# Stores issued from GpSimd, and twelve prepended rows left out of the later stages, in a hybrid decoder layer on one Trainium2 core

## The chip, the cores and the metric

The kernel runs on one core of one Trainium2 chip. A core has four compute engines that run side by side, each with its own in-order queue of instructions: TensorE (PE, matrix products into PSUM), VectorE (DVE), ScalarE (ACT) and GpSimd (POOL). SyncE (SP) computes nothing; it issues DMAs between HBM and SBUF. Engines wait for one another by semaphores. The metric is the device time of one execution in microseconds; several executions are timed and the median is compared.

## The reference, cut to what matters

One layer of a decoder trunk with 1024 channels is applied to a prompt of 2048 rows, preceded by 16 learned "meta" rows, and to 8 sample sequences of 8 rows each with stored histories. All in float32. In short:

```
h    = rmsnorm(x)                       # per row, 1024 channels
z    = h @ w_in                         # 1024 -> 5 x 1024: value, gate, pool input, two merge gates
a    = value * sigmoid(gate)            # then causal depthwise convolution, width 31, layernorm, silu, @ w_conv_out
p    = trailing mean over 2/4/8/16 rows of the pool input, minus the row itself; small products, scale
x    = x + (sigmoid(g_a) * a + sigmoid(g_b) * p) @ w_out
up   = rmsnorm(x) @ w_up                # 1024 -> 2 x 2816, causal depthwise convolution, width 3
x    = x + (gelu(up_gate) * up_value) @ w_down
y    = rmsnorm(x)                       # y_prompt = y[:, 16:], the 16 meta rows are dropped
```

Beside y, the last rows of each history are returned (30 of the width-31 convolution, 15 of the pooling, 2 of the width-3 convolution), for the prompt and for the samples. What a row needs from earlier rows is thus: 30 rows of `a`, 15 rows of the pool input, 2 rows of `up`. The first row of y that is kept is row 16.

## The kernel before

**Layout.** Channels lie on the 128 partitions, in 8 chunks; rows are columns. All rows, 16 + 2048 + 64 = 2128, are cut into three blocks (`NBLK`, `WIDTHS`, lines 33 to 41) of 708, 708 and 712 columns; the 64 sample rows are the last columns of block 2. A block is computed in two halves of `hw(b)` = 354 or 356 columns (lines 229 to 241), since a PSUM bank holds 512 float32 columns.

**Products.** Precision is kept by splitting both operands in a high and a low part: `gemm` (line 331) issues three matmuls for each chunk of 128 input channels and each half, so a unit of 1024 input channels is 8 x 2 x 3 = 48 matmuls. Every matmul goes through the helper at line 212. The up-projections stream two columns more per half (the history of the width-3 convolution). In block 2, 19 of the 22 pairs of up-projections are computed by a recursive scheme with 7 products of half size instead of 8 (`pair`, line 964).

**Weights.** A weight tile is loaded (`raw`), split by ScalarE and VectorE into a tile `wb` with both parts (`w_split`, line 293), and, if a later block needs it, stored to a DRAM tile `keep` (`w_stores`, line 270). Later uses load the split form from `keep` (`w_loads`, line 275). There are four `wb` buffers; a `wb` buffer is loaded or written again when TensorE has read it and its store has landed. The sums and differences of weights that block 2's scheme needs are prepared during block 1 and kept in the same way (`mixed_weights`, line 867: 14 stores for each of 19 pairs).

**Order.** The order of all instructions is written out by the program itself, under `manual_schedule`: a planner (`Pace`, line 71) keeps, for each engine and for the DMA, the time at which it would be free, and every helper reports a cost to it (`pace.put`). The list of units is walked in order; after each unit's matmuls, `drip` (line 1442) lets evacuations, weight splits and tasks (norms, convolutions) issue instructions until VectorE's planned time comes near TensorE's. Some tasks also hold back while the planned DMA time is ahead of TensorE's (`calm`, lines 882 and 1091). Each engine then executes its own instructions in the order in which they were issued.

**Queues.** All loads (line 204) and all stores (line 208) are issued by SyncE, in one queue. GpSimd makes small copies only (`pcopy`, line 200): the last rows of a block into the histories `ahist`, `phist`, `hhist`, and from there to the head of the next block's tiles.

**Stages of a block.** `G` (gate and value inputs), `PG` (pool input, pool products, merge gate), `C` (second merge gate, convolution's output product), `WO` (output projection), `FF` (up-projections with down-projections between them). In `value_post` (line 527) the tile of `a` has its 30 history columns ahead of the block's own; in `pool_post` (line 670) the pool tile has 15. For the first 16 rows the trailing mean is corrected by a table of counts (lines 707 to 710). `final` (line 1085) normalizes and stores y. All 2128 rows go through all stages.

Of the kernel before, what the change touches and what calls it, by code (L numbers as in the profile page):

```python
# [9 lines left out]
F32R = mybir.dt.float32r  # L10
# [4 lines left out]
P = 128  # L15
# [18 lines left out]
SBLK = 2  # L34
TOT = NP_ALL + NSAMP
_W = TOT // NBLK // 4 * 4
# [96 lines left out]
def trunk(ctx: ExitStack, tc: tile.TileContext, A, O):  # L133
# [73 lines left out]
    def store(dst, src):  # L207
        nc.sync.dma_start(out=dst, in_=src)  # L208
        pace.put("dma", size(src) * P * 4 / 340.0, [], [src], late=2000.0)

# [15 lines left out]
    def hcol(o):  # L226
        return half[:, o - O_LG : o - O_LG + 1]

    def hw(b):
        return WIDTHS[b] // 2  # L230

    def cols(b, ts_):
# [7 lines left out]
    def ps_of(ps, b, ts_, off=0):  # L240
        return ps[:, : len(ts_), off : off + hw(b)]

    R = {}
# [100 lines left out]

    def rng(b, ts_, halo=0):
        h = hw(b)
        return [(t * h, (t + 1) * h + halo) for t in ts_]

# [76 lines left out]
    def x_load(b, c, c0=0, c1=None):  # L425
        c1 = WIDTHS[b] if c1 is None else c1
        x = S(c1 - c0)
        load(x, A["x"][c, :, COL0[b] + c0 : COL0[b] + c1])
        return x
# [18 lines left out]
    def norm1_first(ts_):  # L448

        c0, c1 = cols(0, ts_)  # L450
        xs = [x_load(0, c, c0, c1) for c in range(KC)]
        yield at(xs[0])

        def src(c):
            yield
            return xs[c]

        r = yield from rstd_of(src, c1 - c0)
        if ts_[0] == 0:
            R["h", 0] = [(S(WIDTHS[0], F32R), S(WIDTHS[0], F32R)) for _ in range(KC)]  # L460

        def first(c):
            stt(xs[c], xs[c], col(O_N1 + c), r, ALU.mult, ALU.mult)
            act(R["h", 0][c][0][:, c0:c1], xs[c], AF.Copy)
            return xs[c], *(x[:, c0:c1] for x in R["h", 0][c])

        yield from staggered(first)
# [53 lines left out]
    def gate_post(b, c, ts_, ps):  # L521
        if ts_[0] == 0:
            R["t", b, c] = S(WIDTHS[b])
        act(sb(R["t", b, c], b, ts_), ps_of(ps, b, ts_), AF.Tanh, scale=0.5)
        yield

    def value_post(b, c, ts_, ps):
        n, h, t = NPB[b], hw(b), R["t", b, c]
        if ts_[0] == 0:
            a = S(HC + n)  # L530
            pcopy(a[:, :HC], ahist[:, c, :])
            R["a", b, c] = [a, None, 0]
        a = R["a", b, c][0]
        if n == WIDTHS[b]:
            stt(sb(a[:, HC:], b, ts_), sb(t, b, ts_), 1.0, ps_of(ps, b, ts_), ALU.add, ALU.mult)
        else:
            s = R["sa", c]
            stt(a[:, HC : HC + h], t[:, :h], 1.0, ps[:, 0, :h], ALU.add, ALU.mult)
            stt(a[:, HC + h : HC + n], t[:, h:n], 1.0, ps[:, 1, : n - h], ALU.add, ALU.mult)
            new = t[:, n:].rearrange("p (a c) -> p a c", a=NS)  # L540
            stt(new, new, 1.0, ps[:, 1, n - h : h].rearrange("p (a c) -> p a c", a=NS), ALU.add, ALU.mult)
            ts(s[:, :, HC:], new, 0.5, None, ALU.mult)
            store(O["conv_s"][c], s)
            R["a", b, c][1] = 1
        if ts_[-1] == 1:
            pcopy(ahist[:, c, :], a[:, n : n + HC])
            R["a", b, c][2] = 1
            del R["t", b, c]
        yield
# [120 lines left out]
    def pool_post(b, c, ps):  # L670
# [3 lines left out]
        u = S(HP + n)  # L674
        pcopy(u[:, :HP], phist[:, c, :])
        if samp:
# [5 lines left out]
        else:  # L682
            act(sb(u[:, HP:], b, BOTH), ps_of(ps, b, BOTH), AF.Copy)
        pcopy(phist[:, c, :], u[:, n : n + HP])
# [22 lines left out]
        if b == 0:  # L707
            e = mpool.tile([P, 16], F32, tag="e", name=nm("e"), bufs=2)
            tt(e, cur[:, HP : HP + 16], cst[:, O_IC + 16 * g : O_IC + 16 * g + 16], ALU.mult)
            tt(pf[:, :16], e, u[:, HP : HP + 16], ALU.subtract)  # L710
        hi, lo = S(W, F32R), S(W, F32R)
# [420 lines left out]

    def std_unit(w, pairs, b, ts_, post, needs=(), wait=False, halo=0, pre=None, drop=None, hold=None):
        box = []

        def mmf(w):
            if pre:
                pre()
            ps = hold.pop() if hold else PSUM()
            (box if hold is None or ts_ == SECOND else hold).append(ps)  # L1140
            yield from gemm(ps if hold is None else ps[:, ts_[0] :, :], w, pairs(), rng(b, ts_, halo))
            if drop:
                del R[drop]
# [8 lines left out]
    def gate(b, c, w, nd, ts_=BOTH):  # L1152
        std_unit(w, lambda: R["h", b], b, ts_, lambda ps: gate_post(b, c, ts_, ps), nd)

    def value(b, c, w, nd, ts_=BOTH, drop=False):
        std_unit(
            w, lambda: R["h", b], b, ts_, lambda ps: value_post(b, c, ts_, ps), nd,
            pre=past(b, "sa", c, HC, "st_conv", 3), drop=("h", b) if drop else None,
        )
# [44 lines left out]
    def in_unit(b, part, c, post, nd, pre=None, drop=None):  # L1204
        std_unit(
            W(("in", part * KC + c), A["w_in"][part * KC + c]), lambda: R["h", b], b, BOTH, lambda ps: post(b, c, ps), nd, pre=pre, drop=drop
        )
# [391 lines left out]
```

## Time and profile before

| | us |
|---|---|
| median of 3 runs | 3002.06 (3000.92 to 3005.93) |
| the profiled execution's own time | 3004.2 |
| its span, first to last instruction | 3002.1 |

The profile is one execution. Its page shows how long each engine was busy, what ended idle times ("releaser"), the chain of work that ended last, the instructions in groups (out <- in, partitions x elements, count, total and mean time) and the DMA issues with their time to landing. In the names, `ps` is PSUM, `s` a slot of the working pool, `wb` a split weight, `raw` a weight as loaded, `keep` the split weights in DRAM, `xd` block 2's rows that are spilled to DRAM, `in_` and `out_` the kernel's inputs and outputs. PEld is TensorE's loading of the stationary operand, which overlaps its products. SPq is SyncE's queue.

Over the span the core moved 660.41 MB by DMA, 433.35 MB read from HBM and 224.17 MB written, a mean of 220 GB/s; the granted clock of TensorE was 0.993 of full speed on the mean. A matmul's time in the groups is its time from start to end; matmuls overlap, so it is about twice the interval from one to the next.

### The profile page before, as it was taken

How to read it: one execution, taken by the hardware profiler on the slowest of the kernel's cores; microseconds unless marked ns; L12 is line 12 of the kernel's file. 1: busy time of each engine (PE TensorE's matmuls, PEld its weight loads, DVE VectorE, ACT ScalarE, POOL GpSimd, SP SyncE). 2: the span in 40 equal slices, each digit the busy share in tenths (PEclk: the TensorE clock that was granted, in tenths of full speed). 3: DMA queues.
4: the chain of work that ended last, by engine and by line, in shares of the span. 5: the costliest groups of instructions: out<-in, count | busy, mean ns of one | idle time of the engine just before them, and what ended most of it. 6: DMA issues, size and time to landing. Idle time of an engine off the chain costs nothing.

```text
span 3002.1 us, 44205 instructions
## 1 busy us (share of the span) xinstructions
PE 2938.3 (98%) x17928; PEld 2924.6 (97%) x17928; DVE 2042.8 (68%) x3006; ACT 821.2 (27%) x1238; POOL 108.8 (4%) x201
## 2 busy tenths in 40 slices
PE   7999999999999998999999999999999999999998
PEld 7999999999999998999999999999999999999997
DVE  7998998679996456653489999655652137544645
ACT  4201334233223232432221212223241113221312
POOL 0111100020000000000010000000000000000000
PEclk9999999999999999999999999999999999999999
DMA  7424554955655557888743444799743376777686
GB/s 283 160 71 161 196 207 162 335 212 173 229 189 197 204 191 286 274 321 277 277 154 120 163 136 146 266 320 328 266 170 138 139 267 215 255 268 263 236 302 242
DMA packets 187755, 660.41 MB, mean 220 GB/s; under 512 B 30880, under 2 KB 39200, under 8 KB 145696
## 3 DMA queue, kind: packets, MB, share of 16 engines
q1 hardware_dynamic: 187552, 657.59, 62.2%
q8 instruction: 141, 2.31, 0.3%
q14 instruction: 62, 0.51, 0.0%
HBM read 433.35 MB, written 224.17 MB: 219 GB/s over the span
## 4 chain that ended last, share of the span: by engine, by line
PE 81%; DVE 12%; ACT 2%; DMA 2%; issue 2%; SPq 0%; DVEq 0%; ACTq 0%
PE ps L212 81%; DVE s L184 8%; DVE s L180 2%; DVE wb L180 2%; ACT s L195 2%; DMA wb<-keep 1%; DMA s<-in_x 0%; ACT wb L195 0%; DMA out_ffn_s<-sf 0%; DMA raw<-in_w_in 0%; SPq L204 0%; DVE s L189 0%; DMA raw<-in_w_dn 0%; SPq L208 0%; DVE rs L184 0%
## 5 line engine op out<-in xcount | busy, mean ns | idle before, releaser
L212 PE MATMUL ps<-s,wb 128*128 128x356 f32 (+2 forms) x17628 | 2904.4, 326 | 32.3 <-DMA wb<-keep 11.7
L212 PEld LDWEIGHTS ps<-s,wb 128*128 128x128 f32 x17628 | 2886.3, 189 | 43.2 <-DVE s L180 19.4
L184 DVE SCALAR_TENSOR_TENSOR s<-s,half,s 128x708 f32<-128x708 f32 (+1 forms) x720 | 622.5, 928 | 0.0
L195 ACT ACTIVATE s<-s 128x708 fp32r<-128x708 f32 (+8 forms) x447 | 316.2, 715 | 829.9 <-DVE s L184 465.8
L180 DVE TENSOR_TENSOR s<-s,s 128x708 f32<-128x708 f32 (+10 forms) x526 | 402.4, 779 | 102.5 <-ACT s L195 92.7
L180 DVE TENSOR_TENSOR s<-s,ps 128x708 f32<-128x708 f32 (+4 forms) x225 | 159.7, 719 | 289.9 <-PE ps L212 233.5
L195 ACT ACTIVATE s<-ps 128x358 f32<-128x358 f32 (+4 forms) x197 | 117.5, 603 | 696.4 <-PE ps L212 679.8
L184 DVE SCALAR_TENSOR_TENSOR s<-ps,cst,s 128x708 f32<-128x708 f32 (+1 forms) x188 | 179.0, 953 | 91.6 <-ACT s L195 88.0
L184 DVE SCALAR_TENSOR_TENSOR s<-s,cst,s 128x712 f32<-128x712 f32 (+3 forms) x188 | 156.5, 845 | 88.2 <-ACT s L195 81.0
L180 DVE TENSOR_TENSOR wb<-raw,wb 128x1024 fp32r<-128x1024 f32 (+3 forms) x136 | 152.9, 1126 | 41.0 <-ACT wb L195 40.6
L195 ACT ACTIVATE wb<-raw 128x1024 fp32r<-128x1024 f32 (+3 forms) x136 | 132.2, 977 | 157.4 <-PE ps L212 92.3
L195 ACT ACTIVATE s<-ps,cst 128x708 f32<-128x708 f32 (+1 forms) x94 | 79.4, 847 | 272.9 <-PE ps L212 266.5
L184 DVE SCALAR_TENSOR_TENSOR s<-s,ps 128x708 f32<-128x708 f32 (+5 forms) x65 | 43.8, 695 | 144.1 <-PE ps L212 124.8
L184 DVE SCALAR_TENSOR_TENSOR s<-s,s 128x708 f32<-128x708 f32 (+2 forms) x96 | 85.5, 891 | 73.4 <-ACT s L195 71.6
L180 DVE TENSOR_TENSOR s<-raw,s 128x512 fp32r<-128x512 f32 x114 | 74.5, 687 | 60.8 <-ACT s L195 52.5
L195 ACT ACTIVATE s<-raw 128x512 fp32r<-128x512 f32 x114 | 68.2, 626 | 86.9 <-DMA raw<-in_w_up 68.7
L180 DVE TENSOR_TENSOR s<-s 128x722 f32<-128x722 f32 (+6 forms) x64 | 55.3, 863 | 28.2 <-ACT s L195 20.5
L200 POOL COPY s<-phist 128x15 f32<-128x15 f32 x24 | 16.5, 687 | 1080.4 <-PE ps L212 1023.8
L184 DVE SCALAR_TENSOR_TENSOR sc<-sa,cst,sc 128x64 f32<-128x64 f32 x232 | 46.9, 280 | 0.3
L195 ACT ACTIVATE s<-s,half 128x708 f32<-128x708 f32 (+1 forms) x48 | 46.5, 975 | 0.8
L195 ACT ACTIVATE s<-s,cst 128x712 f32<-128x712 f32 x38 | 33.7, 886 | 40.4 <-DVE s L180 38.4
L200 POOL CAST s<-hhist 128x2 fp32r<-128x2 f32 x48 | 17.5, 396 | 607.8 <-PE ps L212 389.8
(51 smaller groups left out, 369.5 us busy)
## 6 DMA issues: line engine op xcount, KB each, us to landing
wb<-keep SPq DMA_DIRECT2D x227, 1024.0 KB, 5.0
keep<-wb SPq DMA_DIRECT2D x100, 1024.0 KB, 6.3
keep<-s SPq DMA_DIRECT2D x266, 256.0 KB, 5.7
raw<-in_w_up SPq DMA_DIRECT2D x82, 512.0 KB, 5.7
wb<-keep SPq DMA_DIRECT2D x40, 640.0 KB, 5.2
wb<-keep SPq DMA_DIRECT2D x32, 768.0 KB, 5.2
raw<-in_w_in SPq DMA_DIRECT2D x40, 512.0 KB, 5.2
s<-in_x SPq DMA_DIRECT2D x40, 354.0 KB, 7.6
```

What stands on the lines that cost most here:

```text
L180: nc.vector.tensor_tensor(out=out, in0=a, in1=b, op=op)
L184: nc.vector.scalar_tensor_tensor(out=out, in0=a, scalar=s, in1=b, op0=op0, op1=op1)
L195: nc.scalar.activation(out, a, func, **kw)
L200: nc.gpsimd.tensor_copy(out, a)
L212: nc.tensor.matmul(out, lhsT=lhsT, rhs=rhs, start=start, stop=stop, skip_group_check=again)
```

## The change

Two edits are made together.

First, `store` issues its DMA from GpSimd in place of SyncE. To the planner a store is now an instruction of GpSimd of 1000 ns whose source is free 2000 ns and the transfer's time later; the DMA's planned time grows by the transfer alone and no longer waits for the store's source.

Second, the first 12 of the 16 meta rows (`SKIP`) go only through what later rows need of them: the gate and value inputs and the pool input of block 0. Of a first row kept in the other stages, row 12, the convolution reaches back 30 rows, so `a` of rows 0 to 11 is still computed; it is written into the history columns ahead of the block's own (`HC - lead(b)`), and the same holds for the pool input. The blocks become 704, 704 and 708 columns wide. Block 0's gate, value and pool units stream both halves of 716 columns, 358 each (`hx`, `rows="all"`); its merge gates start at column 12 of the normalized rows (`rows="h"`).

```diff
-TOT = NP_ALL + NSAMP
+SKIP = 12
+TOT = NP_ALL + NSAMP - SKIP
...
     def store(dst, src):
-        nc.sync.dma_start(out=dst, in_=src)
-        pace.put("dma", size(src) * P * 4 / 340.0, [], [src], late=2000.0)
+        nc.gpsimd.dma_start(out=dst, in_=src)
+        move = size(src) * P * 4 / 340.0
+        pace.put("pool", 1000.0, [], [src], late=2000.0 + move)
+        pace.free["dma"] += move
...
+    def lead(b):
+        return SKIP if b == 0 else 0
+    def hx(b):
+        return (WIDTHS[b] + lead(b)) // 2
+    def sx(ap, b, ts_):
+        return ap[:, ts_[0] * hx(b) : (ts_[-1] + 1) * hx(b)].rearrange("p (a c) -> p a c", a=len(ts_))
+    def px_of(ps, b, ts_):
+        return ps[:, : len(ts_), : hx(b)]
...
-    def rng(b, ts_, halo=0):
-        h = hw(b)
-        return [(t * h, (t + 1) * h + halo) for t in ts_]
+    def rng(b, ts_, halo=0, rows="own"):
+        h = hx(b) if rows == "all" else hw(b)
+        o = lead(b) if rows == "h" else 0
+        return [(o + t * h, o + (t + 1) * h + halo) for t in ts_]
...
     def value_post(b, c, ts_, ps):
-            pcopy(a[:, :HC], ahist[:, c, :])
+            pcopy(a[:, : HC - lead(b)], ahist[:, c, : HC - lead(b)])
...
-            stt(sb(a[:, HC:], b, ts_), sb(t, b, ts_), 1.0, ps_of(ps, b, ts_), ALU.add, ALU.mult)
+            stt(sx(a[:, HC - lead(b) :], b, ts_), sx(t, b, ts_), 1.0, px_of(ps, b, ts_), ALU.add, ALU.mult)
...
     def pool_post(b, c, ps):
-        pcopy(u[:, :HP], phist[:, c, :])
+        pcopy(u[:, : HP - lead(b)], phist[:, c, : HP - lead(b)])
...
-            act(sb(u[:, HP:], b, BOTH), ps_of(ps, b, BOTH), AF.Copy)
+            act(sx(u[:, HP - lead(b) :], b, BOTH), px_of(ps, b, BOTH), AF.Copy)
```

In the same way the loads of x and the normalized tiles of block 0 (`x_load`, `norm1_first`) take the 12 rows in, the table of counts is read from entry 12 on, and `gate`, `value` and the pool inputs pass `rows="all"`, block 0's merge gates `rows="h"`. On the host, x keeps all rows and the output y has 12 rows fewer.

More of the change, by code (lines that the diff above doesn't have):

```diff
@@ L427, in x_load @@
         x = S(c1 - c0)
-        load(x, A["x"][c, :, COL0[b] + c0 : COL0[b] + c1])
+        load(x, A["x"][c, :, SKIP + COL0[b] + c0 : SKIP + COL0[b] + c1])
         return x
@@ L448, in norm1_first @@
     def norm1_first(ts_):
-        c0, c1 = cols(0, ts_)
-        xs = [x_load(0, c, c0, c1) for c in range(KC)]
+        c0, c1 = ts_[0] * hx(0), (ts_[-1] + 1) * hx(0)
+        xs = [x_load(0, c, c0 - SKIP, c1 - SKIP) for c in range(KC)]
         yield at(xs[0])
@@ L459, in norm1_first @@
         if ts_[0] == 0:
-            R["h", 0] = [(S(WIDTHS[0], F32R), S(WIDTHS[0], F32R)) for _ in range(KC)]
+            R["h", 0] = [(S(2 * hx(0), F32R), S(2 * hx(0), F32R)) for _ in range(KC)]
         def first(c):
@@ L522, in gate_post @@
         if ts_[0] == 0:
-            R["t", b, c] = S(WIDTHS[b])
-        act(sb(R["t", b, c], b, ts_), ps_of(ps, b, ts_), AF.Tanh, scale=0.5)
+            R["t", b, c] = S(2 * hx(b))
+        act(sx(R["t", b, c], b, ts_), px_of(ps, b, ts_), AF.Tanh, scale=0.5)
         yield
@@ L708, in pool_post @@
             e = mpool.tile([P, 16], F32, tag="e", name=nm("e"), bufs=2)
-            tt(e, cur[:, HP : HP + 16], cst[:, O_IC + 16 * g : O_IC + 16 * g + 16], ALU.mult)
-            tt(pf[:, :16], e, u[:, HP : HP + 16], ALU.subtract)
+            k = 16 - SKIP
+            tt(e[:, :k], cur[:, HP : HP + k], cst[:, O_IC + 16 * g + SKIP : O_IC + 16 * g + 16], ALU.mult)
+            tt(pf[:, :k], e[:, :k], u[:, HP : HP + k], ALU.subtract)
         hi, lo = S(W, F32R), S(W, F32R)
@@ L1131, in add_task, with std_unit @@
         order.append(t)
-    def std_unit(w, pairs, b, ts_, post, needs=(), wait=False, halo=0, pre=None, drop=None, hold=None):
+    def std_unit(w, pairs, b, ts_, post, needs=(), wait=False, halo=0, pre=None, drop=None, hold=None, rows="own"):
         box = []
@@ L1140, in mmf @@
             (box if hold is None or ts_ == SECOND else hold).append(ps)
-            yield from gemm(ps if hold is None else ps[:, ts_[0] :, :], w, pairs(), rng(b, ts_, halo))
+            yield from gemm(ps if hold is None else ps[:, ts_[0] :, :], w, pairs(), rng(b, ts_, halo, rows))
             if drop:
@@ L1152, in gate @@
     def gate(b, c, w, nd, ts_=BOTH):
-        std_unit(w, lambda: R["h", b], b, ts_, lambda ps: gate_post(b, c, ts_, ps), nd)
+        std_unit(w, lambda: R["h", b], b, ts_, lambda ps: gate_post(b, c, ts_, ps), nd, rows="all")
     def value(b, c, w, nd, ts_=BOTH, drop=False):
@@ L1157, in value @@
             w, lambda: R["h", b], b, ts_, lambda ps: value_post(b, c, ts_, ps), nd,
-            pre=past(b, "sa", c, HC, "st_conv", 3), drop=("h", b) if drop else None,
+            pre=past(b, "sa", c, HC, "st_conv", 3), drop=("h", b) if drop else None, rows="all",
         )
@@ L1205, in in_unit @@
         std_unit(
-            W(("in", part * KC + c), A["w_in"][part * KC + c]), lambda: R["h", b], b, BOTH, lambda ps: post(b, c, ps), nd, pre=pre, drop=drop
+            W(("in", part * KC + c), A["w_in"][part * KC + c]), lambda: R["h", b], b, BOTH, lambda ps: post(b, c, ps), nd, pre=pre, drop=drop,
+            rows="all" if part == 2 else "h",
         )
@@ L1542 @@
     samp = I["x_sample"].reshape(NSAMP, D)
-    cut = sum(NPB[: SBLK + 1])
+    cut = SKIP + sum(NPB[: SBLK + 1])
     x = np.concatenate([prompt[:cut], samp, prompt[cut:]], axis=0)
@@ L1559 @@
     arrays = {
-        "x": x.T.reshape(KC, P, TOT),
+        "x": x.T.reshape(KC, P, SKIP + TOT),
         "cst": cst,
@@ L1582 @@
     y = o["y"].reshape(D, TOT).T
-    yp = np.concatenate([y[N_META:cut], y[cut + NSAMP :]], axis=0)[None]
+    cut -= SKIP
+    yp = np.concatenate([y[N_META - SKIP : cut], y[cut + NSAMP :]], axis=0)[None]
     ys = y[cut : cut + NSAMP].reshape(NS, TS, D)
```

## The prediction

> **What bounds the kernel now.** I read the busy shares first, then the matmul groups by shape, then windows inside single stages, then who waits for whom (TensorE, the DMA queue of SyncE, GpSimd), then the chain of waits around the longest stalls and at the end.
>
> ```profile
> span 3002.1 us, 44205 instructions
> PE 2938.3 (98%) x17928; PEld 2924.6 (97%) x17928; DVE 2042.8 (68%) x3006; ACT 821.2 (27%) x1238; POOL 108.8 (4%) x201
> L212 PE MATMUL ps<-s,wb 128*128 128x356 f32 x8064 | 1327.0, 326 | 7.2 <-ACT s L195 3.1 <-DVE s L184 1.5 <-DVE s L180 1.3
> L212 PE MATMUL ps<-s,wb 128*128 128x354 f32 x7680 | 1265.6, 327 | 14.9 <-DMA wb<-keep 9.6 <-ACT s L195 4.3 <-DVE s L180 1.0
> L212 PE MATMUL ps<-s,wb 128*128 128x358 f32 x1884 | 315.6, 328 | 10.2 <-DVE s L180 8.5 <-DMA wb<-keep 1.7
> ```
>
> TensorE is the bound: 17628 matmuls of 354 to 358 columns, with 64 us of idle time in the whole span. So the change can pay in two ways only: a shorter interval between matmuls, or fewer stalls. The windows below lie inside stages without a stall; their columns are length, busy time with count, granted clock, DMA share and GB/s.
>
> ```profile
> 1200.00:1400.00 200.00, 200.00 (x1229) 1.00 0.88 308
> 2200.00:2410.00 210.00, 210.00 (x1295) 1.00 0.38 139
> 785.00:861.00 76.00, 76.00 (x465) 1.00 0.54 187
> 2774.00:2845.00 71.00, 68.50 (x412) 1.00 0.71 249
> ```
>
> One matmul lasts about 0.326 us and overlaps the next, so the interval is (window + 0.326) over the count: 163.0 ns at 354 columns (block 1's projections), 162.4 at 356 in block 2's projections, 164.1 at 356 in the up-projections of block 0. In the last window, the 358-column products of block 2, 2.5 us are idle and every wait is followed by a refill, so 167 ns is an upper figure.
>
> The stalls that a DMA ends are few:
>
> ```profile
> PE ps L212 <- DVE s L180: 28.0, 24, 10.2
> PE ps L212 <- DMA wb<-keep: 11.7, 4, 7.5
> ```
>
> The longest of them, in the chain of waits, with the two windows that follow it and a window around the second one (windows of all engines: PE, PEld, DVE, ACT, POOL, then clock and DMA):
>
> ```profile
> 1178.97 9.32 DMA wb<-keep
> 1188.29 0.14 issue
> 1188.43 6.67 PE ps L212 x23
> 1184.00:1194.00 10.00, 5.57 (x19) 5.60 (x20) 7.72 (x10) 3.38 (x6) 2.05 (x4) 0.51 1.01 420
> 2111.00:2121.00 10.00, 7.95 (x50) 7.68 (x49) 10.00 (x13) 4.95 (x8) 0.00 (x0) 1.00 1.00 342
> ```
>
> The reader should see two things. The load that TensorE waits for took 9.32 us, and the granted clock fell to 0.51 after the long stall: 23 matmuls took 6.67 us where 23 x 0.163 = 3.7 us is normal, so 2.9 us more were lost. After a stall of about 2 us (second window) the clock stayed at 1.00.
>
> **The change, part by part.**
>
> *Fewer columns.* Blocks go from 708, 708, 712 columns to 704, 704, 708. Blocks 0 and 1 have 3840 matmuls each that go from 354 to 352 columns and 2112 up-projections that go from 356 to 354; block 2 has 3840 from 356 to 354 and 1884 from 358 to 356. Against this, block 0's gate, value and pool inputs keep the 12 rows: 24 units of 48 matmuls, 1152, go from 354 to 358. In columns streamed: 16476 x 2 = 32952 fewer, less 1152 x 4 = 4608 more, 28344 in all. The number of matmuls does not change.
>
> The price of a column is not plain from the trace. From 354 (163.0) to the up-projections' 356 (164.1) it is 0.55 ns; from 354 to block 2's 356 (162.4) it is -0.3 ns; an interval wholly in proportion to its columns gives 163.0/354 = 0.46. I take 0.4, near the last two positive ones: 28344 x 0.4 = **-11.3 us**. Bounds: -0.3 gives +8.5, 0.55 gives -15.6. VectorE and ScalarE lose 4 of 708 columns as well; they are 68% and 27% busy and lie beside the matmuls, so I count nothing.
>
> *Stores leave SyncE's queue.* Waits of that queue, stores being line 208:
>
> ```profile
> SPq L208 <- ACT s L195: 141.3, 73, 5.8
> SPq L208 <- DVE wb L180: 92.9, 10, 15.9
> SPq L208 <- DVE s L180: 87.1, 95, 5.0
> SPq L204 <- PE ps L212: 1141.5, 275, 27.1
> SPq L204 <- DVE wb L180: 685.1, 116, 24.9
> ```
>
> Three groups of stores hold the head of the queue for 321 us in all, and loads stand behind them. But loads (line 204) wait far more for TensorE and for the weight splits, that is, for their own buffers. So most of the head-of-line time is hidden, and what can come back is what TensorE loses to DMA. Around the stalls the queue looks like this (the last two lines are the load of the fourth stall in the chain of waits, and the loads' median time to landing):
>
> ```profile
> 1176.66 1.33 SPq L204 DMA_DIRECT2D raw<-in_w_up  x2
> 1178.04 0.53 SPq L208 DMA_DIRECT2D keep<-wb  x1
> 1178.97 7.24 SPq L204 DMA_DIRECT2D wb<-keep  x4
> 2107.32 1.05 SPq L208 DMA_DIRECT2D keep<-s  x2
> 2108.43 2.77 SPq L204 DMA_DIRECT2D s<-in_x  x4
> 2111.55 7.47 SPq L204 DMA_DIRECT2D wb<-keep  x4
> 2163.23 6.70 SPq L208 DMA_DIRECT2D out_y<-s  x8
> 2170.02 5.38 SPq L204 DMA_DIRECT2D wb<-keep  x3
> 2479.08 6.47 DMA wb<-keep
> wb<-keep SPq DMA_DIRECT2D x227, 1024.0 KB, 5.0
> ```
>
> At 1178.97 the load is issued as its buffer comes free and shares the engines with a 1 MB store and two loads that had stood behind stores; the median landing of such a load is 5.0 us, so 9.32 - 5.0 = 4.3 us can go, and with a shorter stall some of the 2.9 us of slow clock; I take half, 1.5. At 2111 stores held the queue between two groups of x loads, and at 2170 eight stores of y stood ahead of the load. These two and the fourth stall (ended at 2485, beside eight stores of x) hold 11.7 - 7.5 = 4.2 us; I take half, 2.1. Sum: **-7.9 us**. Bounds: 11.7 + 2.9 = -14.6, and on the other side +4.3, if a load that now starts beside a store is held up by as much as the worst one was. What is late next after these stalls is VectorE (28.0 us above), which the change does not touch.
>
> *Stores join GpSimd's queue.* No row shows a DMA issued there. The rows are the two large groups of stores as SyncE issues them (shortest, median and longest issue in ns, first and last start), their landing, a window of block 0, the nearest GpSimd rows, and the end: eight y stores issued in 3.82 us beside the eight VectorE instructions of 4.05 us that feed them.
>
> ```profile
> L208 SPq DMA_DIRECT2D keep<-s x266: 319/408/1999, 1157.0 to 2160.7; - x133
> L208 SPq DMA_DIRECT2D keep<-wb x136: 319/432/1767, 16.3 to 1178.0; - x136
> keep<-wb SPq DMA_DIRECT2D x100, 1024.0 KB, 6.3
> 250.00:500.00 250.00, 250.00 (x1540) 249.56 (x1539) 222.48 (x273) 89.21 (x109) 21.81 (x21) 1.00 0.55 194
> L200 POOL COPY phist<-s 128x15 f32<-128x15 f32 x24 | 19.0, 792 | 238.7 <-ACT s L195 148.2 <-ACT su L195 90.4
> L200 POOL CAST s<-s 128x2 fp32r<-128x2 f32 x16 | 5.3, 355 | 52.2 <-ACT s L195 38.8 <-issue 5.4 <-DVE s L180 4.9
> L200 POOL COPY ahist<-s 128x30 f32<-128x30 f32 x24 | 16.7, 694 | 362.2 <-DVE s L184 362.2
> 2994.94 4.05 DVE L184 SCALAR_TENSOR_TENSOR s<-s,cst,ps 128x356 f32<-128x356 f32 x8 [1.75 <-PE ps L212]
> 2995.55 3.82 SPq L208 DMA_DIRECT2D out_y<-s  x8
> ```
>
> Bounds for one issue: 0.32 us (SyncE's shortest) and 1.4 us (twice a 0.69 us copy); I take 0.8, the row of the 0.79 us copy. The groups of stores of line 208 add up to 529 (the 266 and 136 here and 127 smaller ones), so 529 x 0.8 = 423 us beside the 109 that GpSimd is busy now: it stays under a fifth and is no bound on the mean. At the end nothing hides it: the last eight y stores come every 0.5 us and would leave every 0.8, 8 x 0.3 = 2.4, and with a slower start of the last one I take **+3 us** (bounds 0 and 8 x 0.9 = +7).
>
> Elsewhere a store waits in order behind small copies, and copies behind stores. The copies behind which a store can be stuck longest are those of `ahist`, waiting for VectorE: 362.2 us over 24, 15 us each. The buffers that wait for the stores are the four of `wb`, read by TensorE in units of 48 x 0.163 = 7.8 us; a buffer is written again some three units later, so a store has about 20 us, of which 6.3 go to landing. In block 2's hand-over to the up-projections GpSimd has 16 casts and 8 spill stores, 16 x 0.36 + 8 x 0.8 = 12 us, beside 72 matmuls of the first half, 11.7 us, that hide it. I count **+2 us** for this (bounds 0, and the slower rival below).
>
> Sum against the profiled execution's own time, 3004.2 us (span 3002.1 and 2.1 around it): -11.3 - 7.9 + 3 + 2 = -14.2, so 2990.0. That execution lies 2.1 us above the median of the runs, 3002.06, so the forecast for the median is **2988 us**.
>
> **The rivals.**
>
> *The interval does not follow the columns* (weight loading or a fixed turn sets it). For it: block 2's 356 columns are no slower than 354. Against it: the up-projections in the same block and the 358 group, both slower. Then -7.9 + 3 + 2 = -3: **2999 us**.
>
> *The place of the columns counts, not only their number.* Blocks 0 and 1 now start their second half at column 354, block 2 at 356, a multiple of four; the change swaps this (352 there, 354 here). The two 356-column windows differ by 1.7 ns and differ in just this. Then 10752 matmuls gain 1.7 ns more, 1884 products of block 2 too, and 3840 lose it: -18.3 - 3.2 + 6.5 = -15 beside the forecast: **2973 us**.
>
> *The stalls stay,* because those loads waited for a buffer and then for bandwidth, which stores take from whichever queue. For it: 1141.5 us of loads waiting for TensorE, and DMA shares of 1.00 in the windows of both stalls. Then -11.3 + 3 + 2 = -6.3: **2996 us**. The Trainium skill says so as a rule (DMA: Bandwidth & Descriptors, section "Issuing engines are not separate DMA queues"): DMAs of all issuing engines run on the same 16 engines, and a second one saves only issue time; by it this rival is the likelier. The trace agrees as far as the 1.00 goes, but shows the order of the queue as well.
>
> *Slower: stores come late through GpSimd and hold `wb` buffers.* Place: block 0, where most of the 136 stores of new weights fall and VectorE, 222 of 250 us busy in the window above, keeps `ahist` copies waiting. It decides once a store stands more than the spare 20 - 6.3 = 13.7 us behind a copy. The copies' mean wait is 15 us and the longest 48.9; if five of 24 hold a store 5 us too long, TensorE loses 25 us: -11.3 - 7.9 + 3 + 2 + 25 = +11, **3013 us**. Against it: the program issues a copy at about the time its input is planned, and loads have lived with the same order on SyncE. The Trainium skill adds a cause (SBUF — State Buffer, the box on the "DVE blocks DMA" trap): descriptors of DMAs from GpSimd can't be written while VectorE runs a two-port instruction; no run here shows it so far.
>
> **How the numbers follow.** Forecast 2988 (own range 2980 to 2996): 0.42. Fixed interval, 2999: 0.17. Place of the columns, 2973: 0.11. Stalls stay, 2996: 0.13, half of it on either side of the bound. Late stores, 3013: 0.17. About 0.2% (6 us) is what a measurement of this kernel can tell from no change: faster by more (under 2996) 0.42 + 0.11 + 0.07 = 0.60, within 0.2% 0.17 + 0.06 = 0.23, slower 0.17. The range is 2971 to 3010: it leaves out the upper part of the slower case and the lower edge of the fastest.
>
> **What would show it.** The matmul groups by shape: the 352 group's interval near 162.2 ns and block 0's 358 near 164.6 show the column price; 161 or less at 352 shows the place. TensorE's wait for `wb<-keep` under 5 us and no clock of 0.5 near 1184 show the stalls gone. GpSimd's busy time near 530 us shows 0.8 us per issue; the last y store's issue after the last VectorE instruction shows the tail. The prediction is wrong if new waits of TensorE for a DMA or a split appear in block 0, or if the interval does not move.

## The result, and the profile after

| | before | after |
|---|---|---|
| median, us | 3002.01 (3000.92 to 3005.93) | 2983.88 (2982.72 to 2986.44) |
| ratio of the medians | | 0.9938, 95% interval 0.9921 to 0.9956 |
| the profiled execution's own time | 3004.2 | 2985.0 |
| its span | 3002.1 | 2983.2 |

The time fell by 18.1 us where 14 were forecast. The total is near, but two terms of the sum are far off and cancel in part. From here on the change shifts the lines: a matmul is line 215, a load 205, a store 209, a GpSimd copy 201, a ScalarE operation 196, VectorE's two main forms 181 and 185.

The page after (busy time, share and count of each engine):

```profile
span 2983.2 us, 44492 instructions
PE 2918.1 (98%) x17928; PEld 2906.2 (97%) x17928; DVE 2034.3 (68%) x3006; ACT 817.5 (27%) x1238; POOL 380.2 (13%) x730
```

The matmuls of the changed kernel grouped by shape (busy time, mean ns of one, then idle time before them and its releasers):

```profile
L215 PE MATMUL ps<-s,wb 128*128 128x354 f32 x8064 | 1319.3, 325 | 10.4 <-DMA wb<-keep 6.6 <-ACT s L196 1.4 <-DVE s L181 1.3
L215 PE MATMUL ps<-s,wb 128*128 128x352 f32 x6528 | 1060.7, 324 | 9.9 <-ACT s L196 9.7 <-DVE s L181 0.3
L215 PE MATMUL ps<-s,wb 128*128 128x356 f32 x1884 | 314.9, 328 | 12.3 <-DVE s L181 9.1 <-DMA wb<-keep 3.2
L215 PE MATMUL ps<-s,wb 128*128 128x358 f32 x1152 | 197.3, 332 | 4.0 <-ACT s L196 3.4 <-DVE s L181 0.5
```

The counts by width are the ones that the prediction worked out; TensorE is still 98% busy. The mean of 324 to 332 ns hardly moves, since matmuls overlap; what moved is how many fit into a stretch. Three windows of the changed kernel inside stages without a stall (length, then each engine's busy time with its count, clock, DMA share, GB/s):

```profile
213.00:279.00 66.00, 66.00 (x415) 66.00 (x414) 57.85 (x68) 8.59 (x10) 9.01 (x13) 1.00 0.45 162
1200.00:1400.00 200.00, 200.00 (x1244) 200.00 (x1243) 104.03 (x140) 73.30 (x106) 55.07 (x104) 1.00 0.85 302
2200.00:2400.00 200.00, 200.00 (x1237) 199.97 (x1235) 56.33 (x75) 46.18 (x62) 2.29 (x8) 1.00 0.42 153
```

The second window holds 1244 matmuls of 352 columns where it held 1229 of 354: (200 + 0.326)/1244 = 161.0 ns against 163.0. The first is the clearest place. In the kernel before, the same stretch (block 1's gate and value products) was:

```profile
213.00:279.00 66.00, 66.00 (x407) 66.00 (x406) 56.98 (x66) 8.61 (x10) 7.34 (x10) 1.00 0.40 144
```

407 products of 354 columns, 163.0 ns each, became 415 of 352, 159.8 ns: 3.2 ns for two columns.

To add this up over the span I took from both traces, for each width, the mean of all start-to-start intervals under 222 ns (longer ones are stalls or slow clock) times the number of products:

```
            352            354            356            358           sum, us
before       -        7680 x 162.91  8064 x 163.16  1884 x 164.66   2877.1
after   6528 x 160.73 8064 x 162.31  1884 x 162.35  1152 x 164.14   2853.1
```

**-24.0 us** come from the intervals. The span fell by 18.9, so all the rest together *rose* by 5.1: the time from the start of the last large product to the end of the span went from 13.8 to 16.2, and the excess in stretches of half clock from about 8 to about 12. TensorE's stalls come to about 50 us in both kernels; they, its small products and the start make up the difference, and how it splits between them depends by some 2 us on the way of counting.

GpSimd's two large groups of stores in the changed kernel (busy time, mean ns of one, then idle time before them):

```profile
L209 POOL DMA_DIRECT2D keep<-s x266 | 142.3, 540 | 640.4 <-ACT s L196 507.8 <-DVE s L181 108.1 <-issue 19.3
L209 POOL DMA_DIRECT2D keep<-wb x136 | 77.1, 567 | 690.0 <-DVE wb L181 673.6 <-DVE rs L192 8.4 <-DVE s L185 6.8
```

Who TensorE waits for there (total, times, longest):

```profile
PE ps L215 <- DVE s L181: 23.5, 22, 9.6
PE ps L215 <- ACT s L196: 14.5, 6, 7.2
PE ps L215 <- DMA wb<-keep: 9.8, 4, 4.9
```

An issue costs 0.54 to 0.57 us, not 0.8. The wait for loads seems to have shrunk a little, from 11.7 to 9.8. But the longest stall has only changed its name. The timeline around it (start, length, instruction, idle time before it):

```profile
1161.13 0.54 POOL L209 DMA_DIRECT2D keep<-s  x1 [0.38 <-issue]
1161.80 0.67 POOL L209 DMA_DIRECT2D keep<-wb  x1
1163.95 19.67 SPq L205 DMA_DIRECT2D wb<-keep  x5
1173.06 11.18 PE L215 MATMUL ps<-s,wb 128*128 128x352 f32 x54 [7.24 <-ACT s L196]
```

The 7.24 us are put down to ScalarE, whose last operation ended at 1172.95. The load of the same weights, issued at 1163.95 just behind a store of a split weight from GpSimd (which landed at 1173.70), landed at 1172.93 by its DMA record: 9.0 us, as before (9.32). Both ended within 0.02 us of one another, so this row alone cannot tell which of them was waited for; the experiment with a quiet hand-over, below, does. The stall is the one forecast to shrink, and it did not.

### The profile page after: what moved, and what is told of

Read it like the earlier page. It is cut to its first block, busy times and chain, and to the rows that moved or that the text cites. A ratio compares the mean times of both kernels' runs of the same rounds, so it can differ in the third digit from the quotient of the medians.

```text
span 2983.2 us, 44492 instructions
## 1 busy us (share of the span) xinstructions
PE 2918.1 (98%) x17928; PEld 2906.2 (97%) x17928; DVE 2034.3 (68%) x3006; ACT 817.5 (27%) x1238; POOL 380.2 (13%) x730
## 4 chain that ended last, share of the span: by engine, by line
PE 85%; DVE 6%; issue 3%; DMA 3%; ACT 2%; POOL 1%; SPq 0%; DVEq 0%; POOLq 0%; ACTq 0%
PE ps L215 85%; DVE s L185 4%; DVE s L181 1%; DMA wb<-keep 1%; ACT s L196 1%; DVE wb L181 1%; POOL keep L209 1%; DMA raw<-in_w_in 1%; DMA raw<-in_w_up 0%; DMA s<-in_x 0%; DMA keep<-s 0%; ACT wb L196 0%; DMA raw<-in_w_out 0%; SPq L205 0%; DVE s L190 0%
## 5 line engine op out<-in xcount | busy, mean ns | idle before, releaser
L215 PE MATMUL ps<-s,wb 128*128 128x354 f32 (+3 forms) x17628 | 2885.0, 325 | 36.5 <-ACT s L196 14.5
L185 DVE SCALAR_TENSOR_TENSOR s<-s,half,s 128x704 f32<-128x704 f32 (+1 forms) x720 | 619.6, 925 | 0.0
L196 ACT ACTIVATE s<-s 128x704 fp32r<-128x704 f32 (+10 forms) x447 | 314.6, 711 | 808.2 <-DVE s L185 455.9
L181 DVE TENSOR_TENSOR s<-s,s 128x704 f32<-128x704 f32 (+11 forms) x526 | 400.7, 775 | 98.3 <-ACT s L196 89.9
L181 DVE TENSOR_TENSOR s<-s,ps 128x704 f32<-128x704 f32 (+4 forms) x225 | 158.8, 715 | 288.8 <-PE ps L215 246.8
L196 ACT ACTIVATE s<-ps 128x356 f32<-128x356 f32 (+5 forms) x197 | 117.0, 600 | 683.7 <-PE ps L215 650.7
L185 DVE SCALAR_TENSOR_TENSOR s<-ps,cst,s 128x704 f32<-128x704 f32 (+1 forms) x188 | 178.2, 949 | 110.9 <-ACT s L196 107.2
L209 POOL DMA_DIRECT2D keep<-s x266 | 142.3, 540 | 640.4 <-ACT s L196 507.8
L185 DVE SCALAR_TENSOR_TENSOR s<-s,cst,s 128x708 f32<-128x708 f32 (+4 forms) x188 | 156.0, 842 | 88.0 <-ACT s L196 82.0
L185 DVE SCALAR_TENSOR_TENSOR s<-s,s 128x704 f32<-128x704 f32 (+2 forms) x96 | 85.2, 888 | 70.9 <-ACT s L196 68.2
```

The lines of the kernel that those rows point to most:

```text
L181: nc.vector.tensor_tensor(out=out, in0=a, in1=b, op=op)
L185: nc.vector.scalar_tensor_tensor(out=out, in0=a, scalar=s, in1=b, op0=op0, op1=op1)
L196: nc.scalar.activation(out, a, func, **kw)
L209: nc.gpsimd.dma_start(out=dst, in_=src)
L215: nc.tensor.matmul(out, lhsT=lhsT, rhs=rhs, start=start, stop=stop, skip_group_check=again)
```

## The experiments

Every ratio is against runs of the kernel before on the same chip; brackets are 95% intervals. First, the two halves of the change by themselves, and the queue apart from the planner's account of it.

**Stores alone.** The kernel before, with the whole of the new `store`; all 2128 rows go everywhere.

```diff
-        nc.sync.dma_start(out=dst, in_=src)
-        pace.put("dma", size(src) * P * 4 / 340.0, [], [src], late=2000.0)
+        nc.gpsimd.dma_start(out=dst, in_=src)
+        move = size(src) * P * 4 / 340.0
+        pace.put("pool", 1000.0, [], [src], late=2000.0 + move)
+        pace.free["dma"] += move
```

> The kernel before with its stores issued from GpSimd and planned as in the change; all 2128 rows stay. Theory A (the gain of 18 us is all in the matmul intervals, about -22 us, and moving the stores costs about 3 us, most of it at the end): 3002 + 3 = 3005 us, steady intervals as before (163.0 ns at 354 columns), stalls for wb<-keep still about 10 us. Theory B (the steps of the forecast: columns about -11, stalls -8, tail and queue +5): about 2999 us, stalls under 5 us.

Measured: 3006.50 us, ratio 1.0015 [1.0006, 1.0024]: about 5 us slower. The stalls stayed: TensorE waits 15.0 us for loads of weights where it waited 11.7, and the longest of these waits is 6.6 us where it was 7.5. About 2 us of the loss lie at the end, where the time from the start of the last large product went from 13.8 to 15.9.

**Rows alone.** The changed kernel with the old `store`.

```diff
-        nc.gpsimd.dma_start(out=dst, in_=src)
-        move = size(src) * P * 4 / 340.0
-        pace.put("pool", 1000.0, [], [src], late=2000.0 + move)
-        pace.free["dma"] += move
+        nc.sync.dma_start(out=dst, in_=src)
+        pace.put("dma", size(src) * P * 4 / 340.0, [], [src], late=2000.0)
```

> The changed kernel with its stores put back on SyncE and planned as before; the 12 rows stay left out. Theory A: 2984 - 3 = 2981 us, intervals as in the changed kernel (about 160.9 ns at 352, 162.3 at 356). Theory B: 3002 - 11 = 2991 us.

Measured: 2985.22 us, 0.9945 [0.9933, 0.9958]. Nearly the whole gain of the change is here. The two halves do not add up: +4.9 and -16.4 make -11.5, together they gave -18.1. So the stores' edit costs time in one kernel and next to nothing in the other. Nor do the rows keep all that the intervals give them: by the sum used above these fell by 24.9 us here (to 2852.2), but TensorE stands 4.6 us near 2157 and 2.2 us near 551, where the kernel before has no stall over 1.1 us. The stores' edit has two parts, and the next run separates them.

**Only the queue back.** The changed kernel, with the new account and thus the new order of VectorE's, ScalarE's and TensorE's instructions, but the DMA issued by SyncE.

```diff
-        nc.gpsimd.dma_start(out=dst, in_=src)
+        nc.sync.dma_start(out=dst, in_=src)
```

> The changed kernel with the one call in store put back on SyncE, but planned as a GpSimd store: TensorE, VectorE and ScalarE get the very instructions of the changed kernel in the same order, only the queue of the stores differs. Theory A: the end comes 2.4 us earlier and the stalls stay near 18 us: about 2981 us. Theory B (the queue of SyncE held loads back): stalls grow by about 8 us: about 2990 us.

Measured: 2977.73 us, 0.9917 [0.9903, 0.9930]. GpSimd's queue, which the change introduces, *costs* about 6 us (the two 95% intervals, 0.9921 to 0.9956 with it and 0.9903 to 0.9930 without, just overlap, so the size is rough; where the time goes is traced below); the new account, at 2985.22 - 2977.73 = 7.5 us, pays. Where it pays most is seen in the chain of waits at about 900 us, in the kernel with rows alone (where a matmul is line 213) and then in this one:

```profile
895.40 0.90 DVE s L181
896.30 0.14 issue
896.44 8.63 PE ps L213 x37
```

```profile
875.00 30.14 PE ps L215 x183
```

With the old account the chain runs over VectorE from 875 to 896, TensorE stands 4.9 us, and 37 products then take 8.63 us where 37 x 0.163 = 6.0 is normal. With the new one TensorE is never without work there. The account changes when the planner hands VectorE's instructions out; no queue is involved.

**The account alone, all rows.** The kernel before with the new account and stores on SyncE.

```diff
-        pace.put("dma", size(src) * P * 4 / 340.0, [], [src], late=2000.0)
+        move = size(src) * P * 4 / 340.0
+        pace.put("pool", 1000.0, [], [src], late=2000.0 + move)
+        pace.free["dma"] += move
```

> The kernel before (all 2128 rows, stores on SyncE) with the planner's new account of a store alone; against e1_stores_only only the queue of the stores differs, the other engines' instructions are the same. Theory (the queue costs 4 to 6 us here as well): 3001 us. Rival (the queue is free, and e1's loss came from the new plan): 3006 us.

Measured: 3001.54 us, 1.0004 [0.9995, 1.0013]; the stall at 901 is still 4 us long. So the account is worth nothing with the old widths and 7.5 us with the new ones; its worth hangs on how VectorE's work happens to fall in one place. The queue seems to cost here too: 0.11% by the two ratios (1.0015 and 1.0004), 3 us, and 5 by the two medians; each ratio is uncertain by 0.09%, so by itself this is not clear of noise.

Next, why the intervals fell by twice what the columns should give.

**Other widths, all rows.** The kernel before with block widths that all have halves of a multiple of four.

```diff
-WIDTHS = [_W + 4 * (i >= NBLK - (TOT - NBLK * _W) // 4) for i in range(NBLK)]
+WIDTHS = [704, 712, 712]
```

> The kernel before with blocks of 704, 712 and 712 columns in place of 708, 708 and 712: same rows, same matmuls, same columns in total, stores on SyncE; now every half starts at a multiple of four columns (352, 356, 356). If the interval follows the number of columns alone: 3002 us, within 3. If the start of the second half counts too, as the intervals of 163.0 ns at 354 and 162.5 at 356 in the kernel before suggest: block 0 at about 160.9, block 1 at 162.5 instead of 163.0: about -11 us, 2991 us.

Measured: 2990.32 us, 0.9961 [0.9948, 0.9973]: 11 us gained with not one row left out, 10.3 of them in the intervals (2866.8 by the sum used above). Two windows of it; the first has 356 columns (block 1), like the second:

```profile
213.00:279.00 66.00, 66.00 (x408) 66.00 (x407) 58.03 (x67) 8.62 (x10) 7.28 (x10) 1.00 0.43 151
1200.00:1400.00 200.00, 200.00 (x1229) 200.00 (x1228) 103.81 (x138) 74.15 (x106) 4.31 (x7) 1.00 0.86 297
```

356 columns are no slower than 354 were (407 and 1229). The step lies between 352 and 354.

**Poor places, the same columns in total.** The kernel with only the queue back, with halves of 350, 354 and 354 columns.

```diff
-WIDTHS = [_W + 4 * (i >= NBLK - (TOT - NBLK * _W) // 4) for i in range(NBLK)]
+WIDTHS = [700, 708, 708]
```

> The kernel of e3_same_plan_sync with blocks of 700, 708 and 708 columns: same rows and columns, but all halves are now 350 or 354 wide, so no second half starts at a multiple of four columns, except the 356-column gate, value and pool inputs of block 0. If the place counts: block 1 back at 163.0 ns (+9 us), its up-projections +2, block 0 about 0: 2978 + 10 = 2988 us. If the number of columns alone counts: 2978 us, within 3.

Measured: 2987.99 us, 0.9955 [0.9942, 0.9967], 10 us more than with 352, 352 and 354, for the same 2116 rows; 6.7 of them lie in the intervals (2861.6 against 2854.9). By columns alone nothing should have changed. Most of the rest is the stall near 898, which is back with 4.9 us although the new account is in force: the account removes it with one set of widths and not with another. And with blocks of 704, 712 and 712 columns the old account leaves only 1.1 us of it.

```profile
213.00:279.00 66.00, 66.00 (x408) 66.00 (x407) 55.43 (x65) 8.59 (x10) 8.00 (x10) 1.00 0.40 145
1200.00:1400.00 200.00, 200.00 (x1228) 200.00 (x1227) 102.98 (x137) 71.96 (x105) 2.91 (x7) 1.00 0.86 295
```

These are products of 354 columns again, and the counts are those of the kernel before.

**Same columns, moved by two.** These widths change the number of columns and their place together. One more run changes the place alone: block 1's normalized rows are written two columns into their tiles for the gate and value products (they pass `rows="gv"` in this run), and four columns in for its other input products, as a control.

```diff
+        if b == 1 and rows != "own":
+            o = 2 if rows == "gv" else 4
         return [(o + t * h, o + (t + 1) * h + halo) for t in ts_]
...
-            hi, lo = S(W, F32R), S(W, F32R)
-            act(hi, x, AF.Copy)
+            o = 0 if b != 1 else 4 if last else 2
+            hi, lo = S(W + o, F32R), S(W + o, F32R)
+            act(hi[:, o:], x, AF.Copy)
             h.append((hi, lo))
-            return x, hi, lo
+            return x, hi[:, o:], lo[:, o:]
```

> The changed kernel with all stores on SyncE and its planner's account (as before: 2977.7 us), and block 1's normalized rows written two columns into their tiles for the gate and value products (768 matmuls of 352 columns between 102 and 280 us, so that the halves start at columns 2 and 354) and four columns in for the other input products (1536 between 1137 and 1397 us, starts 4 and 356). Columns, counts and the order of every engine stay. The unshifted intervals are 159.7 ns and 161.1 ns. Theory (a product costs as many groups of four columns as its columns touch, about 2 ns for a group): the first group of products goes to 161.7 to 162.8 ns, 405 to 410 matmuls in the window from 213 to 279 us in place of 415, and the second stays at 161 ns; in all 1.5 to 2.4 us. Rival (the column count alone sets the interval, and the fast 352 was a matter of the number): both stay, 415 in the window. Rival (only the start of the second half counts, as the prediction had it): half of the theory's gain is lost, about 161 ns, 411 to 412 in the window.

Windows of the gate and value products and of the control, moved and (second fence) not moved:

```profile
213.00:279.00 66.00, 66.00 (x407) 66.00 (x406) 55.42 (x64) 8.58 (x10) 8.08 (x10) 1.00 0.41 147
1290.00:1340.00 50.00, 50.00 (x313) 50.00 (x312) 22.15 (x31) 13.18 (x21) 0.00 (x0) 1.00 0.97 336
```

```profile
213.00:279.00 66.00, 66.00 (x415) 66.00 (x414) 57.84 (x68) 8.59 (x10) 8.25 (x10) 1.00 0.42 151
1290.00:1340.00 50.00, 50.00 (x312) 50.00 (x311) 22.95 (x32) 12.61 (x20) 0.00 (x0) 1.00 0.96 334
```

352 columns from column 2 on take as long as 354 did from column 0 on: 407 in the window, 163.0 ns, so both rivals fall. Moved by four, nothing like it happens. The mean over all 768 went from 159.7 to 163.0 ns, a little more than the 162.8 that the theory gave as its upper end; over the 1536 of the control from 161.1 to 160.6. In one execution the 2.5 us that this adds do not show in the time (2977.19); they are read from the intervals.

So a product's interval follows, in the main, the number of groups of four columns that its columns touch. With second halves starting at column 354, 354 columns touch 89 groups, as 356 do from column 356 on; 352 columns touch 88 groups from 0, 4 and 352 on, and 89 from 2 and 354 on. A group costs 2.0 ns (163.0 - 161.0 in the window from 1200) to 3.2 ns (window from 213). The two runs with other widths fit: counted in this way, halves of 352, 356 and 356 columns touch 3840 groups fewer than those of the kernel before (one for each product of block 0 but the up-projections), and halves of 350, 354 and 354 touch 2688 more than 352, 352 and 354 (one for each of these products in block 1, less one for each of the 1152 wider ones in block 0; those of the up-projections cancel in both); the 10.3 and 6.7 us found in the intervals are 2.7 and 2.5 ns a group. The Trainium skill has a cause that fits (SBUF — State Buffer, section "Specifications (TRN2)"): SBUF is read in lines of 16 bytes, and each step to a new line costs something; four float32 values are 16 bytes. That a line is what counts here is inferred; that the place counts is shown. The rule is not exact. Block 2's products of 354 columns run at 162.0 ns (1237 in the window from 2200) beside 162.4 for 356 before, where both touch 89 groups. Taken by halves, the 354 columns of the window from 1200 need 162.5 ns from column 0 on and 163.6 from column 354 on in the kernel before, and 162.2 and 164.2 with poor places, though each touches 89 groups: the start has a part of its own that the count leaves out. And 352 columns from the same places take 159.8 ns in one window and 161.0 in the other; what makes that difference between the stages stays open.

Last, what GpSimd's queue costs and where. With stores on SyncE, the spill of block 2's rows before its up-projections looks like this in the timeline, then in the DMA issues from 2446 to 2466 (KB each, median us to landing):

```profile
2455.80 8.31 SPq L209 DMA_DIRECT2D xd<-s  x8
2460.76 2.19 PE L215 MATMUL ps<-s,wb 128*128 128x356 f32 x12 [0.50 <-DMA wb<-keep]
```

```profile
wb<-keep SPq DMA_DIRECT2D x3, 1024.0 KB, 4.9
```

And in the changed kernel, the same two views and a window (engines, clock, DMA share, GB/s):

```profile
2447.92 0.54 POOL L209 DMA_DIRECT2D xd<-s  x1
2449.43 8.15 SPq L205 DMA_DIRECT2D wb<-keep  x3
2465.55 3.90 PE L215 MATMUL ps<-s,wb 128*128 128x356 f32 x12 [2.87 <-DMA wb<-keep]
```

```profile
wb<-keep SPq DMA_DIRECT2D x4, 1024.0 KB, 8.3
```

```profile
2464.00:2476.00 12.00, 10.45 (x41) 10.48 (x42) 2.37 (x12) 0.57 (x2) 0.00 (x0) 0.57 0.28 115
```

On SyncE the eight spills stand behind weight loads that wait for TensorE (26 of the 46 us from 2430 on), leave from 2455.8 on, and so stay out of the way of the loads before them, which land in 4.9 us. On GpSimd each leaves when its rows are ready, the first at 2440.7 and the third at 2447.9; the DMA share, taken every 5 us from 2445 to 2460, is 0.94 to 1.04, where it is 0.73 to 0.81 with stores on SyncE. The loads then take 8.3 us, TensorE stands 3 us, and the granted clock is 0.57 from 2464 to 2476. The order in the queue, which the prediction counted as a hindrance, had given the loads the right of way. The Trainium skill's rule that the DMAs of all issuing engines share the same 16 engines, and that issuing from several saves only issue time (DMA: Bandwidth & Descriptors, section "Issuing engines are not separate DMA queues") holds, with one addition from these rows: one queue also keeps an order.

**Spills back on SyncE.** The changed kernel, with block 2's spill stores (32 of the 529, the eight above among them) issued by SyncE again.

```diff
-    def store(dst, src):
-        nc.gpsimd.dma_start(out=dst, in_=src)
+    def store(dst, src, q=None):
+        (q or nc.gpsimd).dma_start(out=dst, in_=src)
...
-        store(R["xd", b, c], R.pop(("x1", b, c)))
+        store(R["xd", b, c], R.pop(("x1", b, c)), nc.sync)
```

> The changed kernel with block 2's spill stores alone (xd, 32 of the 529) put back on SyncE; plan, and the orders of TensorE, VectorE and ScalarE, unchanged. Theory: on GpSimd the spills leave as soon as their rows are ready and take bandwidth from the weight loads at block 2's hand-over; on SyncE they stand behind those loads. Then the 3.0 us stall near 2466 and the half clock after it go: 2984 - 5 = 2979 us. Rival: GpSimd's queue costs a little everywhere, and the spills are no special case: 2983 us, stall still there.

Measured: 2981.47 us, 0.9941 [0.9928, 0.9955], where the changed kernel had 0.9938 [0.9921, 0.9956]: 2.4 us less by the medians, no gain by the ratios, so none that is clear of noise. Yet the stall of 3.0 us has shrunk to 1.9 us (ending at 2460), and the stretch of half clock behind it is gone. The end shows where the time went. Span and the end of the chain of waits here, then in the changed kernel, then with all stores on SyncE, then before:

```profile
core 0 of [0], span 2979.7 us
2965.94 2.97 DVE s L185 x6
```

```profile
2974.74 2.97 DVE s L185 x6
2977.73 0.54 POOL out_y L209
```

```profile
core 0 of [0], span 2977.2 us
2970.88 2.96 DVE s L185 x6
```

```profile
2996.02 2.98 DVE s L184 x6
```

From the end of VectorE's last instruction to the end of the span it is 3.1 us before (3002.1 - 2999.0), 3.4 with all stores on SyncE, 5.5 in the changed kernel and 10.8 here. The last y lands at 2972.2 in this run, and GpSimd's closing drain, a record without a row in these views, runs from 2969.30 to 2978.89. It had not been expected, and its 5.3 us more at the end eat the gain.

**Spills and block 2's y on SyncE.** As the run before, and in `final`:

```diff
-            store(O["y"][c, :, COL0[b] + c0 : COL0[b] + c1], x)
+            store(O["y"][c, :, COL0[b] + c0 : COL0[b] + c1], x, nc.sync if b == NBLK - 1 else None)
```

> The changed kernel with two groups of stores back on SyncE: the spills of block 2's rows and block 2's y; the order of VectorE, ScalarE and TensorE is unchanged. Theory (GpSimd's share of the price is the half clock by the spills plus the late end): with spills alone on SyncE the time was 2981.5, with 9.6 us of GpSimd's own drain at the end; if that drain only waits for late stores of its own queue, it is over before the end now, the tail from the last large product is 14 us as with all stores on SyncE, and the time is 2973 to 2978. Rival (the drain is long whatever was stored last): 2981, with GpSimd's drain still the last to end.

Measured: 2976.79 us, 0.9915 [0.9901, 0.9928]: the price of GpSimd's queue is gone (all stores on SyncE gave 0.9917), and the other stores, among them all 402 of weights, cost nothing there that shows. The drain takes 8.2 us in this run also, but from 2920.4 on, right behind GpSimd's last work, where nothing waits for it; it ends at 2928.5, while the last store of its queue had landed at 2923.9. So the drain is not a wait for late stores alone, as the theory had it; it is hidden or not by where the last store of that queue lies. What fills it stays open.

**A quiet hand-over.** The kernel with only the queue back; the task that prepares sums of weights issues nothing from the end of block 0's or 1's up-projections to the third pool unit of the next block.

```diff
-        return posts + ws + [t for t in rest if not (quiet and t.name[0] in ("cv", "sc") or norm and t.name[0] == "mw")]
+        hand = any(mark["up_end", b] <= now["i"] < mark["PG", b + 1] + 3 for b in range(NBLK - 1))
+        return posts + ws + [t for t in rest if not (quiet and t.name[0] in ("cv", "sc") or (norm or hand) and t.name[0] == "mw")]
```

> The kernel of e3_same_plan_sync with one more condition for the task that prepares block 2's weights: it issues nothing between the last down-projections of a block and the third unit of the next. That takes its loads and stores out of the hand-over near 1171. If the 8 us stall there is shared bandwidth: the load lands in about 6 us in place of 10, stall 4 us or less, half clock shorter: 2978 - 6 = 2972 us. If the load is late because its buffer comes free late: 2978 us.

TensorE's wait for loads in the kernel with only the queue back, and in this one:

```profile
PE ps L215 <- DMA wb<-keep: 14.6, 4, 7.8
```

```profile
PE ps L215 <- DMA wb<-keep: 7.7, 6, 3.6
```

Measured: 2967.78 us, 0.9888 [0.9875, 0.9902], 9 to 10 us less than with only the queue back. The stall at 1170 fell from 8.0 to 3.8 us and the one at 2152 vanished. The load in the chain of waits (from 1140 to 1195), without and then with the quiet hand-over:

```profile
1161.23 9.57 DMA wb<-keep
```

```profile
1163.58 5.39 DMA wb<-keep
```

The timeline of this run at that place:

```profile
1169.11 11.14 PE L215 MATMUL ps<-s,wb 128*128 128x352 f32 x51 [3.65 <-DMA wb<-keep]
...
1171.76 0.79 ACT L196 ACTIVATE s<-s 128x704 fp32r<-128x704 f32 x1 [3.00 <-DVE s L185]
```

TensorE starts when the load has landed, 2.65 us ahead of the start of the ScalarE operation that ended at 1172.95 in the changed kernel; so that operation is not what the products need, and there, too, it was the load that was waited for. This is the stall that the prediction had put down to stores ahead of the load in a queue. It yields when the task's loads and stores are moved out of the way, and did not yield when the stores changed queues. The load itself became shorter, 5.4 us for 9.6, and was not issued sooner, so its buffer is not the cause; it shared the DMA engines with other transfers. The DMA share was 1.04 to 1.07 from 1150 to 1160 without the condition and is 0.29 to 0.83 with it. The condition also moves two loads of 512 KB from ahead of this load to behind it; how much is due to these two and how much to the stores, the run does not separate.

**Both.** The same, with spills and block 2's y on SyncE and all other stores on GpSimd.

> The same, and the task that prepares weight sums issues nothing in the hand-over from block 1's down-projections to block 2. Theory (what is left of GpSimd's stores then costs nothing, and the hand-over is worth the 10 us it was worth with all stores on SyncE): 2964 to 2968, no slower than all stores on SyncE with the quiet hand-over (2967.8). Rival (stores of split weights on GpSimd still cost some us by taking bandwidth earlier): 2970 or more.

Measured: 2965.82 us, 0.9882 [0.9868, 0.9895]. That beats both kernels of this study; against the quiet hand-over with all stores on SyncE it cannot be told apart.

## Why the prediction was right, and where it was wrong

*The direction was right; that the total is near is in part luck, since errors of the terms partly cancel.* Forecast -14.2 on the profiled execution's own time, measured 3004.2 - 2985.0 = -19.2.

*Fewer columns, -11.3: mis-sized; the intervals gave -24.0.* The counts were right; the price of a column, 0.4 ns, was averaged over widths that did not differ in columns alone. The view that spoke against it was in the prediction: 356 columns were no slower than 354 in block 2. The rival that took this seriously (the place of the columns) put the term at -11.3 - 15 = -26, and the runs with other widths and with moved columns show that it had the right cause. Its price of 1.7 ns had less behind it than it says: the two windows of 356 columns that it compares differ in their stage as well, and stages alone differ by 1.2 ns (159.8 and 161.0 above). It was wrong in one part: block 2's projections, which go to poorer places, were to lose 6.5 us and lost nothing. The kernel before has no product of 352 columns, so its trace could not show the step below 354.

*Stores leaving SyncE's queue, -7.9: this step failed.* It read the order of issue around four stalls and took about half of what TensorE lost there as the queue's doing. The rival "the stalls stay" was right: the load at 1164 took 9.0 us although the stores had left its queue, and another, at 2143, took 10.5 us and held TensorE for 5.1. The unfavourable bound, "a load that now starts beside a store is held up", +4.3, came true at 2466 with 3 us of stall and slow clock behind it.

*What is late next: VectorE, "which the change does not touch": wrong.* It was touched through the planner's account and the widths: the 4.4 us stall at 901, a wait for VectorE, went away with the new widths and the new account together. With these widths the account was worth 7.5 us, and no part of the sum had it.

*GpSimd's issue, 0.8 us: too dear; 0.54* for each size of store, and 380 us of busy time in place of 530. *Tail, +3: near in size, by luck.* From VectorE's last instruction to the end 3.1 became 5.5, +2.4. But the slow issue that was to cause it did not occur: eight issues are as fast as VectorE feeds them; the time went to GpSimd's closing drain instead.

*GpSimd's queue elsewhere, +2: too small, and wrong in cause.* Of the about 6 us that the queue costs, 2.4 are the tail, which leaves about 4. The spills were said to be hidden since 12 us of GpSimd's work stand beside 11.7 us of matmuls. The work was hidden; the bytes were not.

*Late stores in block 0: did not occur.* TensorE waits 0.9 us in all for a split weight, as before, and a 1 MB store lands in 6.4 us in the median against 6.3. Nothing here bears out that VectorE's activity holds back GpSimd's DMAs; whether VectorE used the form of instruction that the prediction's warning is about, no run shows.

Taken together, the two rivals' terms, -26.3 + 3 + 2 = -21.3, would have given 2981 us.

## What to carry to other kernels

Count a product's moving operand (the one that streams, here the rows) in groups of four float32 columns touched, start included, before pricing a column: here 352 columns moved by two cost as much as 354. Before moving stores to another queue, ask whether the queue's order is a hindrance or a right of way for the loads; here a stall at full DMA share yielded when transfers were moved out of its way, not when they were moved to another queue. A planner's changed account is a change of its own: test it with the DMAs left in their queue.

## What was not expected of the hardware

- Halves of 352 columns starting at columns 2 and 354 instead of 0 and 352: 163.0 ns for 159.7, with the products and their order unchanged.
- A store issued by GpSimd takes 0.54 us of that engine whether it moves 256 KB or 1 MB (0.54 for 256 KB, 0.57 on the mean of the stores of up to 1 MB).
- GpSimd's closing drain lasted 4.3 us in the changed kernel, 9.6 us with the spills alone on SyncE, and 8.2 us in the two kernels with block 2's y there as well; with all stores on SyncE no such wait ends the span. What sets its length stays open.
- Around stalls of 3 to 7 us (2466, 2154, 1173 in the changed kernel) the granted clock was half for 3.4 to 10.2 us, around one of 2.6 us (554) for 6.8; around one of 1.9 us (2460, spills on SyncE) it was not, and around one of 2.0 us at the same place (spills and y on SyncE) it was, for 3.4. The length of the stall alone does not set the length of the slow stretch.
